# One 512-column matmul of the high weights on high and low tokens side by side, for the MLP up and FFN gate and up products of two transformer blocks

## The chip, the cores and the metric

The kernel runs on one NeuronCore of a Trainium2 chip. The metric is the device time of one execution in microseconds (us), smaller is better. TensorE (PE; its weight loads are listed as PEld), VectorE (DVE), ScalarE (ACT), GpSimd (POOL) and the DMA queues (SP issues nearly all weight loads) work side by side, each through its own instructions in program order, and wait for each other by semaphores.

## What is computed

Two blocks in a row on 256 tokens of width 1024, everything in float32. The first block has two layers, each an attention and a squared-ReLU MLP; the second has a SwiGLU feed-forward (FFN), a hybrid mixer and a second FFN.

```python
# first block, for each of 2 layers (D = 1024, F = 4096)
h = h + merge_heads(attention(...)) @ w_o
h = h + jnp.square(jax.nn.relu(rms_norm(h, g) @ w_up)) @ w_down
# second block (F2 = 2816); sh, sc, g: rows of c_act @ w_ada + b_ada (9 of them)
h = modulate(rmsnorm(x, n1), sh1, sc1)
x = x + 0.5 * g1 * ((jax.nn.silu(h @ w_gate) * (h @ w_up)) @ w_down)      # FFN 1
x = x + g2 * hybrid_mixer(modulate(rmsnorm(x, n2), sh2, sc2), ...)
x = x + 0.5 * g3 * (swiglu with other weights of the same shapes)          # FFN 2
return rmsnorm(x, norm_final)
```

## The kernel before

**Products.** Every float32 operand is split into two float32r parts, high and low, and a product is made in three passes that add up in one PSUM bank: high by high, high weights by low tokens, low weights by high tokens. `by_token` (L216, with `part`, L209) gives the result by token: the tokens stand still in the array and 512 columns of weights move, three matmuls of 512 columns for each block of 128 rows. `by_feature` (L233) gives it transposed: 128 columns of the weights stand still and the 256 tokens move, three matmuls of 256 columns (L245, L246, L247) for each block of rows k and each 128 columns n.

**MLP and FFN.** `hidden` (L799) goes through the hidden columns in cuts. For cut j, `up` makes the hidden activations; then the down products of cut j-1 follow (`by_token`), so that one cut's activations are made by the other engines while PE multiplies the one before. The MLP has 8 cuts of 512 columns (L415). After the up product of a cut, for each of its two banks: ScalarE's ReLU (L839), VectorE's square (L841), ScalarE's high part (L259), VectorE's low part (L260). The FFN has a cut of 512 columns made by token, one of 256, and four of 512 (L416); for each bank ScalarE makes the SiLU of the gate (L1092), VectorE the product with the up part (L1102), and then high (L259) and low part (L260).

**Weights.** `plan` lists all weight slabs (128 partitions x 1024 values, 512 KB) in the order of their use. SP loads them into 5 raw buffers. `prepare` (L155) splits each: ScalarE writes the high part (L174, or L178 with a gain for the MLP's up weights), VectorE (for some slabs GpSimd) the low part (L175, L179), into 5 pairs of buffers; PE frees those, the split frees the raw buffer. `take(i)` (L184) emits, at the place where the program uses slab i, the splitting of up to four slabs behind it. So up to four slabs behind the one in use are split ahead, and the instructions that make a cut's hidden activations stand in the queues of ScalarE and VectorE behind the splitting of the slabs of the down products that follow, and ahead of that of the next cut's up slabs. Between the slabs stand 72 slabs of `w_ada` for the second block's modulation, spread over the two MLPs and FFN 1 and 2 at a rate per slab (`plan_hidden`, L400): VectorE adds each up in two instructions (L485), and GpSimd adds over the partitions after every fourth (L490).

**PSUM.** Two pools of four banks: `acc` (down products, projections) and `mm` (up products, transposes, attention).

**Side chains.** Small chains of work (`start`, `tick`) go on between the products; `setup2` (L944) loads small inputs through GpSimd's queue and, 12 ticks later, transposes them (`fill_columns`, L907).

Below, M0 and M1 are the two MLPs, F1 and F2 the two FFNs.

Of the kernel before, what the change touches and what calls it, by code (L numbers as in the profile page):

```python
# [16 lines left out]
S = 256  # L17
# [4 lines left out]
TP = 128  # L22
# [6 lines left out]
def kernel(ctx: ExitStack, tc: tile.TileContext, a: dict, out: bass.AP):  # L29
# [28 lines left out]
    BUFS = {"x": 4, "q": 12, "m": 10, "ra": 3, "rb": 6, "pr": 3, "pT": 4, "gm": 3, "rr": 1}  # L58
# [75 lines left out]
    def load_ahead(most=RB):  # L134
        while at["dma"] < min(len(plan), at["prep"] + most):
# [12 lines left out]
            else:  # L148
                # the first product waits for no more than it needs
# [34 lines left out]
    def take(i):  # L184
        """Slab i, and more made ready behind it."""
# [19 lines left out]
    def by_t(xT, t):  # L205
        """The stationary operands of token tile t: [(hi, lo)] by k."""
        return [(x[0][:, j, tok(t)], x[1][:, j, tok(t)]) for x in xT for j in range(4)]

    def part(p, xs, ws, first, last):  # L209
        """p += x @ w, by token."""  # L210
# [5 lines left out]
    def by_token(idx, xs, ps, first=True, last=True, token_first=False, after=None, before=None):  # L216
        """ps[t] += x[t] @ slab; xs[t]: [(hi, lo)] by k."""
# [15 lines left out]
    def by_feature(idx, xT, ps, before=None):  # L233
        """ps: [128, 2, 256] each; (x @ w)^T, by blocks of 128 columns of w."""
        k = 0
        for i in idx:
            if before is not None:
                before(k)
            for wh, wl in take(i):
                xh, xl = (z[:, k % 4, :] for z in xT[k // 4])  # L240
# [30 lines left out]
    def transposed(bl, tag):  # L271
        """Up to 4 [128, 128] blocks, transposed and split; returns [(hi, lo)] by block."""
# [27 lines left out]
    def mean_square(parts, n, eps=EPS):  # L300
        """mean of squares along the free axis, plus eps."""
# [18 lines left out]
    def warm(func):  # L320
        """Has ScalarE load the table of a function ahead of its use."""
# [9 lines left out]
    def log1p_of(e, shape):  # L331
        """log(1 + e) for 0 <= e <= 1, as 2 atanh(e / (2 + e))."""
# [23 lines left out]
    def columns(n, parts, queue):  # L356
        """Rows of 128 values as columns: [128, n]."""
# [15 lines left out]
    def keep_warm(n):  # L373
        """TensorE's clock is at half speed until it has been busy for some microseconds."""
# [25 lines left out]
    def plan_hidden(ups, w_down, cuts, rate, early=0, after=0):  # L400
        """Weights of the cuts of a hidden layer; each cut's last product is one step behind its first ones."""
        up, down = [], []
        for j in range(len(cuts) + 1):
# [5 lines left out]
            if j > 0:  # L409
                c0, n = cuts[j - 1]  # L410
# [1184 lines left out]
```

## Time and profile before

| | us |
|---|---|
| median of 3 runs | 1217.19 |
| lowest, highest | 1216.63, 1222.46 |
| span of the profiled execution | 1219.5 |
| PE busy in it | 1174.3 (96%) |
| DVE, ACT, POOL busy | 865.2, 650.9, 304.3 |
| DMA queue of the weights, share of 16 engines | 59.7% |

The page gives one profiled execution: its span, the busy time of each engine, the span in slices, the chain of work that ended last, and the costliest groups of instructions. Matmuls overlap in the array, so a matmul's listed duration is longer than its share of the time; what one costs is read from the distance between starts. The order of stages in the span is attention 0 (to 130), M0 (130 to 318), attention 1, M1 (446 to 628), F1 (631 to 822), the mixer, F2 (1022 to 1211).

### The profile page before, as it was taken

Reading aid. Unit: us, or ns where it says so; the run is one execution under the profiler, and the core shown is the slowest. Engines: PE = TensorE matmul, PEld = TensorE weight load, DVE = VectorE, ACT = ScalarE, POOL = GpSimd, SP = SyncE. Lnnn points to the kernel's source line nnn. Section 1 sums busy time; section 2 is a strip of 40 time slices with the busy share of each in tenths; the row PEclk is TensorE's granted clock in tenths of the full one; section 3 lists DMA queues with packets and bytes.
Section 4 is the critical chain, followed back from the end, with each engine's and each line's share of the span. In section 5 each row is a group of like instructions: output and inputs, shape, how many; then the busy total and the mean of one; then the engine's idle time right before and its main releaser. Section 6 shows DMA issues by size and latency. Waiting matters only on the chain.

```text
span 1219.5 us, 19985 instructions
## 1 busy us (share of the span) xinstructions
PE 1174.3 (96%) x7669; PEld 1059.2 (87%) x7669; DVE 865.2 (71%) x1218; ACT 650.9 (53%) x1115; POOL 304.3 (25%) x260
## 2 busy tenths in 40 slices
PE   8999999999999999999989999998998999999997
PEld 8977989988899789989878999988987787899996
DVE  6665678887677568778777877756776776766445
ACT  6565665445555665455545444545765564444443
POOL 3054202133002511211153112154136405111002
PEclk9999999999999999999989999999998999999999
DMA  8642467886553347878846888853632263777650
GB/s 277 194 127 99 157 226 236 274 275 223 184 172 123 105 130 235 288 264 299 284 143 214 292 268 312 276 176 118 220 89 88 93 226 111 270 232 228 222 189 36
DMA packets 128479, 243.04 MB, mean 199 GB/s; under 512 B 8515, under 2 KB 16612, under 8 KB 128384
## 3 DMA queue, kind: packets, MB, share of 16 engines
q1 hardware_dynamic: 126688, 239.96, 59.7%
q0 software_dynamic: 1376, 1.28, 0.5%
q8 instruction: 60, 0.98, 0.3%
q10 hardware_dynamic: 320, 0.53, 0.1%
q14 instruction: 35, 0.29, 0.1%
HBM read 240.65 MB, written 1.09 MB: 198 GB/s over the span
## 4 chain that ended last, share of the span: by engine, by line
PE 64%; DVE 16%; ACT 6%; DMA 6%; issue 5%; POOL 3%; SPq 0%; POOLq 0%; ACTq 0%; DVEq 0%
PE mm L247 8%; PE mm L246 8%; PE mm L245 8%; PE acc L212 7%; PE acc L213 7%; PE acc L214 7%; DVE wl L179 4%; DMA raw<-in_w_down_dram 3%; PE acc L245 3%; PE acc L247 3%; PE acc L246 3%; DVE wl L175 2%; ACT wh L174 2%; PE mm L213 2%; PE mm L212 2%
## 5 line engine op out<-in xcount | busy, mean ns | idle before, releaser
L174 ACT CAST wh<-raw 128x1024 fp32r<-128x1024 f32 (+1 forms) x231 | 237.7, 1041 | 221.0 <-DMA raw<-in_w_down_dram 67.2
L175 DVE TENSOR_TENSOR wl<-raw,wh 128x1024 fp32r<-128x1024 f32 (+1 forms) x193 | 257.8, 1350 | 137.2 <-ACT wh L174 134.8
L247 PE MATMUL mm<-xh,wl 128*128 128x256 f32 x1088 | 309.3, 284 | 4.4 <-DVE wl L179 4.3
L245 PE MATMUL mm<-xh,wh 128*128 128x256 f32 x1088 | 309.1, 284 | 0.1
L246 PE MATMUL mm<-xl,wh 128*128 128x256 f32 x1088 | 308.4, 283 | 0.0
L179 DVE SCALAR_TENSOR_TENSOR wl<-raw,cols,wh 128x512 fp32r<-128x512 f32 (+1 forms) x270 | 204.0, 806 | 68.0 <-ACT wh L178 64.5
L247 PEld LDWEIGHTS mm<-xh,wl 128*128 128x128 f32 x1088 | 209.3, 192 | 5.9 <-DVE wl L179 5.9
L245 PEld LDWEIGHTS mm<-xh,wh 128*128 128x128 f32 x1088 | 209.3, 192 | 1.3 <-ACT wh L178 0.6
L246 PEld LDWEIGHTS mm<-xl,wh 128*128 128x128 f32 x1088 | 209.3, 192 | 0.7
L178 ACT ACTIVATE wh<-raw,cols 128x512 fp32r<-128x512 f32 (+1 forms) x270 | 175.3, 708 | 64.5 <-PE acc L246 20.1
L212 PE MATMUL acc<-wh,mh 128*128 128x512 f32 x524 | 207.6, 396 | 0.0
L213 PE MATMUL acc<-wl,mh 128*128 128x512 f32 x524 | 205.4, 392 | 0.0
L214 PE MATMUL acc<-wh,ml 128*128 128x512 f32 x524 | 205.1, 391 | 0.0
L490 POOL PARTITION_ALL_REDUCE ada<-ada x18 | 66.4, 3690 | 352.1 <-DVE ada L485 153.4
L175 POOL TENSOR_TENSOR wl<-raw,wh 128x1024 fp32r<-128x1024 f32 (+1 forms) x38 | 91.4, 2407 | 138.9 <-ACT wh L174 132.3
L214 PEld LDWEIGHTS acc<-wh,ml 128*128 128x128 f32 x524 | 99.0, 189 | 21.1
L212 PEld LDWEIGHTS acc<-wh,mh 128*128 128x128 f32 x524 | 98.9, 189 | 20.8 <-issue 1.7
L213 PEld LDWEIGHTS acc<-wl,mh 128*128 128x128 f32 x524 | 99.1, 189 | 19.0 <-DVE wl L175 0.2
L485 DVE SCALAR_TENSOR_TENSOR ada<-raw,c_act,ada 128x512 f32<-128x512 f32 x144 | 107.7, 748 | 2.5
L245 PE MATMUL acc<-xh,wh 128*128 128x256 f32 x352 | 102.0, 290 | 0.0
L246 PE MATMUL acc<-xl,wh 128*128 128x256 f32 x352 | 99.5, 283 | 0.0
L247 PE MATMUL acc<-xh,wl 128*128 128x256 f32 x352 | 99.5, 283 | 0.0
(318 smaller groups left out, 1673.5 us busy)
## 6 DMA issues: line engine op xcount, KB each, us to landing
raw<-in_w_ada_dram SPq DMA_DIRECT2D x72, 512.0 KB, 5.4
raw<-in_w_up_dram SPq DMA_DIRECT2D x64, 512.0 KB, 4.9
raw<-in_w_down_dram SPq DMA_DIRECT2D x64, 512.0 KB, 5.7
raw<-in_ffn_w_gate_dram SPq DMA_DIRECT2D x44, 512.0 KB, 4.7
raw<-in_ffn_w_up_dram SPq DMA_DIRECT2D x44, 512.0 KB, 4.7
raw<-in_ffn_w_down_dram SPq DMA_DIRECT2D x44, 512.0 KB, 5.2
raw<-in_moba_w_qkv_dram SPq DMA_DIRECT2D x23, 512.0 KB, 5.0
raw<-in_w_in_dram SPq DMA_DIRECT2D x20, 512.0 KB, 4.1
```

The source lines that it names most:

```text
L174: ACT.copy(hi, raw)
L175: (POOL if i in on_pool else DVE).tensor_tensor(lo, raw, f(hi), op=OP.subtract)
L178: ACT.mul(hi[:, k], raw[:, k], gain[k])
L179: DVE.scalar_tensor_tensor(out=lo[:, k], in0=raw[:, k], scalar=gain[k], in1=f(hi[:, k]), op0=OP.mult, op1=OP.subtract)
L212: PE.matmul(p, lhsT=xh, rhs=wh, start=first and n == 0, stop=False)
L213: PE.matmul(p, lhsT=xh, rhs=wl, start=False, stop=False)
L214: PE.matmul(p, lhsT=xl, rhs=wh, start=False, stop=last and n == len(ws) - 1)
L245: PE.matmul(o, lhsT=wh[:, c], rhs=xh, start=k == 0 and n % 2 == 0, stop=False)
L246: PE.matmul(o, lhsT=wh[:, c], rhs=xl, start=False, stop=False)
L247: PE.matmul(o, lhsT=wl[:, c], rhs=xh, start=False, stop=k == 7 and n % 2 == 1)
L485: DVE.scalar_tensor_tensor(out=acc, in0=raw[:, i, :], scalar=c_act[:, k:k + 1], in1=acc, op0=OP.mult, op1=OP.add)
L490: POOL.partition_all_reduce(acc, acc, TP, ReduceOp.add)
```

## The change

MLP and FFN cuts use a new `by_halves` in place of `by_feature`: high and low tokens lie side by side in one tile, so that one matmul of 512 columns multiplies the high weights with both, into both halves of a whole bank; a matmul of 256 columns adds the low weights by high tokens to the second half. The two halves are added when they are read (`sums`): ScalarE copies the second half to SBUF, VectorE adds the first to it, for 128 hidden columns at a time. A product of 512 columns so needs four banks in place of two. Around it:

- the MLP's square and the FFN's product of gate and up move to GpSimd, and ReLU and SiLU read SBUF;
- the FFN's cuts after the first are all of 256 columns (nine), so that gate and up fit the four `mm` banks; their slabs are 4 blocks of 256 columns; the down products of the last two cuts are made together (`hidden_order`);
- the first cut of an MLP and the second of an FFN use `acc` banks;
- `setup2` starts in attention 0 and transposes when M0 begins.

```diff
-    BUFS = {"x": 4, ...}
+    BUFS = {"x": 2, ...}
...
+    def by_halves(idx, xT, ps, before=None):
+        k = 0
+        for i in idx:
+            if before is not None:
+                before(k)
+            for wh, wl in take(i):
+                x = xT[k // 4][:, k % 4]
+                for n, p in enumerate(ps):
+                    c = slice(n * TP, (n + 1) * TP)
+                    PE.matmul(p, lhsT=wh[:, c], rhs=x, start=k == 0, stop=False)
+                    PE.matmul(p[:, 1, :], lhsT=wl[:, c], rhs=x[:, 0, :], start=False, stop=k == 7)
+                k += 1
+                if k % 2:
+                    tick()
+            done(i)
+            tick()
+
+    def sums(ps, name):
+        got = []
+        for i in range(0, len(ps), 2):
+            u = sb("ra", (TP, 2, S), name=name)
+            for j in range(2):
+                ACT.copy(u[:, j, :], ps[i + j][:, 1, :])
+            for j in range(2):
+                DVE.tensor_tensor(u[:, j, :], ps[i + j][:, 0, :], u[:, j, :], op=OP.add)
+            got.append(u)
+        return got
...
     def new_xT():
-        return [pair("x", (TP, 4, S)) for _ in range(2)]
+        return [sb("x", (TP, 4, 2, S), F32R, "xT") for _ in range(2)]
...
+    def hidden_order(cuts):
+        n = len(cuts)
+        if cuts[-1][1] == 512:
+            return [[j - 1] if j else [] for j in range(n + 1)]
+        return [[j - 1] if 0 < j < n - 2 else [] for j in range(n - 1)] + [[n - 3], [n - 2, n - 1]]
...
-    FFN_CUTS = [(0, 512), (2560, 256)] + [(j * 512, 512) for j in range(1, 5)]
+    FFN_CUTS = [(0, 512)] + [(512 + j * 256, 256) for j in range(9)]
...
     def mlp(...):
-            ps = [mm_ps((TP, 2, S)) for _ in range(2)]
+            ps = [(mm_ps if j else acc_ps)((TP, 2, S)) for _ in range(4)]
...
-            by_feature(ids[0], xT, ps, before)
+            by_halves(ids[0], xT, ps, before)
...
-            for p in ps:
-                r = sb("ra", (TP, 2, S), name="relu")
-                ACT.activation(out=r, in_=p, func=AF.Relu)
+            for u in sums(ps, "up"):
                 q = sb("rb", (TP, 2, S), name="sq")
-                DVE.tensor_tensor(q, r, p, op=OP.mult)
+                ACT.activation(out=u, in_=u, func=AF.Relu)
+                POOL.tensor_tensor(q, u, u, op=OP.mult)
                 hT += hidden_part(q)
...
     def ffn(...):
+            banks = acc_ps if j == 1 else mm_ps
+            ps = [banks((TP, 2, S)) for _ in range(2)]
+            by_halves(ids[0], xT, ps)
+            sg, = sums(ps, "sg")
+            ACT.activation(out=sg, in_=sg, func=AF.Silu)
...
+            ps = [banks((TP, 2, S)) for _ in range(2)]
+            by_halves(ids[1], xT, ps)
             finish(*pending)
+            u, = sums(ps, "up")
+            q = sb("rb", (TP, 2, S), name="gu")
+            POOL.tensor_tensor(q, sg, u, op=OP.mult)
+            return hidden_part(q)
...
-    attention_layer(0, A0, xT, vs, chains, nxt[3])
+    attention_layer(0, A0, xT, vs, chains, nxt[3], lambda: start(setup2()))
```

## Rows read from the trace of the kernel before

**Rows 1.** The page's head: span and instructions, busy us of each engine (share).

```profile
span 1219.5 us, 19985 instructions
PE 1174.3 (96%) x7669; PEld 1059.2 (87%) x7669; DVE 865.2 (71%) x1218; ACT 650.9 (53%) x1115; POOL 304.3 (25%) x260
```

**Rows 2.** Timeline of PE, one cut of M0: start us, us, engine, line, operands.

```profile
209.63 0.28 PE L245 MATMUL mm<-xh,wh 128*128 128x256 f32 x1
...
221.15 0.40 PE L212 MATMUL acc<-wh,mh 128*128 128x512 f32 x1
...
232.05 0.28 PE L245 MATMUL mm<-xh,wh 128*128 128x256 f32 x1
```

**Rows 3.** Costliest groups: xcount, then busy us, mean ns, idle before.

```profile
L245 PE MATMUL mm<-xh,wh 128*128 128x256 f32 x1088 | 309.1, 284 | 0.1
```

**Rows 4.** Windows of M0 (two), F1, F2: length, then busy us by engine.

```profile
209.60:232.10 22.50, 22.50 (x146) 20.57 (x145) 19.52 (x25) 11.90 (x18) 3.17 (x3) 1.00 0.79 269
255.20:279.40 24.20, 23.07 (x145) 20.43 (x143) 19.48 (x24) 11.43 (x18) 4.51 (x2) 1.00 0.79 261
...
744.70:778.60 33.90, 33.90 (x241) 32.05 (x240) 27.98 (x31) 16.05 (x19) 4.93 (x3) 1.00 0.88 311
...
1132.10:1166.00 33.90, 33.90 (x241) 32.04 (x240) 17.26 (x16) 14.71 (x16) 0.00 (x0) 1.00 0.62 200
```

**Rows 5.** Waits of PE, 232 to 300 (M0), then 480 to 606 (M1).

```profile
PE mm L247 <- DVE wl L179: 3.5, 4, 1.7
...
PE mm L247 <- DVE wl L179: 0.8, 2, 0.5
```

**Rows 6.** Timeline of DVE: first square of cuts 2 and 6, M0, then M1.

```profile
178.36 0.68 DVE L841 TENSOR_TENSOR sq<-relu,mm 128x512 f32<-128x512 f32 x1
...
275.44 0.68 DVE L841 TENSOR_TENSOR sq<-relu,mm 128x512 f32<-128x512 f32 x1
...
492.88 0.68 DVE L841 TENSOR_TENSOR sq<-relu,mm 128x512 f32<-128x512 f32 x1
...
589.45 0.68 DVE L841 TENSOR_TENSOR sq<-relu,mm 128x512 f32<-128x512 f32 x1
```

**Rows 7.** Timeline of DVE: the hidden activations of one cut of M0.

```profile
225.47 0.68 DVE L841 TENSOR_TENSOR sq<-relu,mm 128x512 f32<-128x512 f32 x1
226.84 0.70 DVE L260 TENSOR_TENSOR ml<-sq,mh 128x512 fp32r<-128x512 f32 x1 [0.69 <-ACT mh L259]
...
229.43 0.75 DVE L485 SCALAR_TENSOR_TENSOR ada<-raw,c_act,ada 128x512 f32<-128x512 f32 x1
```

**Rows 8.** Groups by form: the nearest operations to the new ones (busy us, mean ns).

```profile
L839 ACT ACTIVATE relu<-mm 128x512 f32<-128x512 f32 x32 | 19.0, 593 | 3.8 <-PE mm L247 3.8
L259 ACT CAST mh<-sq 128x512 fp32r<-128x512 f32 x32 | 19.9, 621 | 37.0 <-DVE sq L841 37.0
L259 ACT CAST mh<-mm 128x256 fp32r<-128x256 f32 x18 | 6.3, 374 | 11.6 <-PE mm L641 9.4 <-PE mm L265 2.1
L260 DVE TENSOR_TENSOR ml<-mm,mh 128x256 fp32r<-128x256 f32 x18 | 7.1, 417 | 17.9 <-ACT mh L259 17.9
L542 POOL TENSOR_TENSOR pr<-pr,rs 128x512 f32<-128x512 f32 x24 | 24.9, 1042 | 89.6 <-DVE rs L541 89.6
```

**Rows 9.** Timeline, F1: gate-by-up products of two cuts; PE's end of the latter cut.

```profile
736.13 0.67 DVE L1102 TENSOR_TENSOR gu<-sg,mm 128x512 f32<-128x512 f32 x1
...
771.73 0.68 DVE L1102 TENSOR_TENSOR gu<-sg,mm 128x512 f32<-128x512 f32 x1
...
767.73 0.40 PE L212 MATMUL acc<-wh,mh 128*128 128x512 f32 x1
```

**Rows 10.** Groups by form, DVE, 682 to 800 (F1): idle before, and on whom.

```profile
L175 DVE TENSOR_TENSOR wl<-raw,wh 128x1024 fp32r<-128x1024 f32 x43 | 59.2, 1395 | 22.8 <-ACT wh L174 22.7
```

**Rows 11.** Timeline of POOL: a step of attention 0; the first load of `setup2`.

```profile
98.70 1.03 POOL L542 TENSOR_TENSOR pr<-pr,rs 128x512 f32<-128x512 f32 x1
...
130.36 0.60 POOL L946 DMA_DIRECT2D b_ada<-in_b_ada_dram  x1 [0.29 <-POOL b_ada L945]
```

More of the change, by code (lines that the diff above doesn't have):

```diff
@@ L205, in by_t @@
     def by_t(xT, t):
-        return [(x[0][:, j, tok(t)], x[1][:, j, tok(t)]) for x in xT for j in range(4)]
+        return [(x[:, j, 0, tok(t)], x[:, j, 1, tok(t)]) for x in xT for j in range(4)]
     def part(p, xs, ws, first, last):
@@ L239, in by_feature @@
             for wh, wl in take(i):
-                xh, xl = (z[:, k % 4, :] for z in xT[k // 4])
+                xh, xl = (xT[k // 4][:, k % 4, e, :] for e in range(2))
                 for n in range(2 * len(ps)):
@@ L402, in plan_hidden @@
         up, down = [], []
-        for j in range(len(cuts) + 1):
+        for j, made in enumerate(hidden_order(cuts)):
             mixed["rate"] = rate if after < j < len(cuts) - 1 else 0.0
@@ L408, in plan_hidden @@
                            for i, (w, g) in enumerate(ups)])
-            if j > 0:
-                c0, n = cuts[j - 1]
+            if made:
+                c0, n = cuts[made[0]][0], sum(cuts[i][1] for i in made)
                 down.append([slab(w_down, c0, n // TP, s * 512, 512) for s in range(2)])
@@ L653, in heads_attention, with attention_layer @@
         return run()
-    def attention_layer(layer, ids, xT, vs, chains, next_chain):
+    def attention_layer(layer, ids, xT, vs, chains, next_chain, between=lambda: None):
         rstd, rrow = [], []
@@ L802, in hidden @@
         acc = [[None, None], [None, None]]
-        made = None
+        made = []
         ups, downs = plans
-        for j in range(len(cuts) + 1):
-            new = up(j, ups[j]) if j < len(cuts) else None
+        downs = list(downs)
+        for j, some in enumerate(hidden_order(cuts)):
+            if j < len(cuts):
+                made.append(up(j, ups[j]))
             if j == 1:
                 acc = [[acc_ps() for _ in range(2)] for _ in range(2)]
-            if 0 < j < len(cuts):
+            if not some:
+                continue
+            hT = sum((made[i] for i in some), [])
+            down = downs.pop(0)
+            if downs:
                 for s in range(2):
-                    apart = tail is not None and j == len(cuts) - 1 and s == 1
-                    by_token(downs[j - 1][s], by_block(made), [acc[t][s] for t in range(2)], first=j == 1,
-                             last=(lambda t, n: t == 1 and n == len(downs[j - 1][s]) - 1) if apart else False)
-            elif j == len(cuts):
+                    apart = tail is not None and len(downs) == 1 and s == 1
+                    by_token(down[s], by_block(hT), [acc[t][s] for t in range(2)], first=some[0] == 0,
+                             last=(lambda t, n: t == 1 and n == len(down[s]) - 1) if apart else False)
+            else:
                 if tail is not None:
                     update(1, 1, acc[1][1])
-                token_first(downs[j - 1], by_block(made), acc, False, lambda t, s: update(t, s, acc[t][s]),
-                            order, tail)
-            made = new
+                token_first(down, by_block(hT), acc, False, lambda t, s: update(t, s, acc[t][s]), order, tail)
     def mlp(layer, plans, xT, vs, chains, next_chain, between=lambda j: None, order=BY_HALF):
@@ L855, in forget_bias @@
         for k in range(8):
-            xh, xl = (z[:, k % 4, :] for z in xT[k // 4])
+            xh, xl = (xT[k // 4][:, k % 4, e, :] for e in range(2))
             PE.matmul(p, lhsT=wf[0][:, k], rhs=xh, start=k == 0, stop=False)
@@ L913, in fill_columns @@
             r += m
-        yield 12
+        if go is None:
+            yield 12
+        else:
+            while not go:
+                yield 1
         p = mm_ps((TP, r))
```

29 lines of the change are left out of this document (7 added, 22 removed).

## The prediction

> **What bounds the kernel now.** I began with the page's head. PE is busy for 1174.3 of 1219.5 us and the other engines far less [rows 1], which looks as if any PE time saved were saved for good. But matmuls overlap, so a busy PE may still be held up, and the average covers stages of several kinds. So I read PE's timeline next: in an ordinary cut of M0 the 96 up matmuls take 221.15 - 209.63 = 11.52 us, 0.1200 us each, and the 48 down matmuls 232.05 - 221.15 = 10.90 us, 0.2271 us each [rows 2]. A cut is 22.4 us of PE.
>
> Then the windows: in M0 VectorE is busy for 19.5 of such a cut's 22.5 us, and a later cut takes 24.2 us [rows 4]. PE's waits say why: from 232 to 300 it waits for VectorE's low parts of the up weights, in M1 a little too [rows 5]. The square of the first bank of a cut is a mark that VectorE passes once a cut. From cut 2 to cut 6 of M0 it takes (275.44 - 178.36) / 4 = 24.27 us a cut, in M1 (589.45 - 492.88) / 4 = 24.14 [rows 6]. PE needs 22.4. So in both MLPs the preparation of weights (load, ScalarE, VectorE, back to the raw buffer) is slower than PE by 1.8 us a cut. It lives on the slabs that it has ahead, and PE waits when these are used up. In F1 the mark is the gate-by-up product: 771.73 - 736.13 = 35.6 us for a cut of 512 columns, of which PE needs 33.9; at 771.73 VectorE is 4.0 us behind PE's end of that cut, and PE does not wait yet [rows 4, 9]. In F2 VectorE is busy for 17.3 of 33.9 us and PE alone sets the pace [rows 4]. The reader should see from this that M0, M1 and F1 have two limits nearly equal, and that a change which takes from PE and gives to VectorE's chain is paid where the chain is late.
>
> **The change part by part.** *Matmuls.* A pair of one row block and 128 columns costs 3 x 0.1200 = 0.3600 us; the new one 0.2271 + 0.1200 = 0.3471, so 0.0129 less [rows 2]. There are 1088 such pairs in the MLPs and FFNs [rows 3]: 256 in M0, 256 in M1, 288 in each FFN's columns after the first cut (8 x 4 x 8; 9 x 2 x 8 for gate and for up). The work of PE falls by 14.0 us: 3.3, 3.3, 3.7, 3.7. No row shows a matmul of 512 followed by one of 256 on the same bank for long; between the two shapes the starts keep their distance [rows 2], so I take the sum of the two.
>
> Here the Trainium skill speaks against the change: the page TensorE: Matmul & The Clock Gate, in the section on why the gap is 56 and not 53.3 ns, has a fixed cost of about 2.5 ns for each warm matmul beyond its columns. By it the edit would save an estimated 1088 x 2.5 ns = 2.7 us of PE's work. The rows differ: 512 columns cost 0.2271 and 256 cost 0.1200, which is 0.1071 for 256 columns and 0.0129 besides [rows 2], and the measurement decides.
>
> *The hidden chain of the MLP.* Now, from the first square to the next instruction of other work, VectorE spends 229.43 - 225.47 = 3.96 us on a cut, waiting 0.69 us for each of two high parts [rows 7]. After the change it makes four adds of 256 columns first. Priced by the 128x256 subtraction from PSUM, 0.417 us, they last 1.67, and ScalarE's copies (128x256 cast, 0.374) run ahead of them while VectorE still splits a slab. The first ReLU waits for the second add: 0.83 + 0.59 = 1.42. Then GpSimd squares (nearest: the 128x512 product, 1.04): 2.46; high part 0.62: 3.08; low part 0.69: 3.77. ScalarE is in order, so the second ReLU follows the first high part: 3.08 + 0.59 = 3.67; square 4.71; high 5.33; low 6.02 [rows 7, 8]. VectorE's chain grows from 3.96 to 6.02, by 2.06 us a cut, though its busy time hardly grows. Queued behind its low parts are the sums for `w_ada` and the splitting of the next cut's up slabs, and PE waits for these. The load waits that VectorE has now come late in a cut, after more than five slabs, so the five raw buffers filled meanwhile do not cover the new wait. The bounds are +0.5 (ScalarE and GpSimd quicker than their nearest rows, waits partly absorbed) and +3 us a cut (each hop of a semaphore, and GpSimd behind a reduction).
>
> From cut 2 on the chain sets the pace: five chains until the first up slab of cut 7, 5 x 2.06 = 10.3 us later than now. PE arrives earlier by 3 cuts x 32 pairs x 0.0129 = 1.2, which only lengthens its wait, but the chain, which starts from PE's end of a cut, starts that much earlier; cut 7 itself gives 0.4. M0: +8.7 us. M1 by the same working: +8.7. With the bounds: 0 to +13 each.
>
> *The FFN's chain.* Now a bank costs VectorE two instructions and a wait, the same 0.68 + 0.69 + 0.60, 1.97 us. After: two adds for the gate, 0.83; two for up, 0.83; square's place taken by the product 1.04; high 0.62; low 0.69: 4.01 [rows 7, 8], that is +2.04 for each cut of 256. SiLU now waits for VectorE's adds, and the next high part of a slab for SiLU: 0 to 0.59 + 1.05 more. Against this, from 682 to 800 VectorE is idle for 22.8 us ahead of its splitting, for ScalarE that waits for loads [rows 10], and with a pause twice in six or seven loads five raw buffers can cover most of it. I take +0.4 a cut, bounds 0 and +3.7. The chain is slower than PE by (35.6 - 33.9) / 2 = 0.85 a cut of 256 already, PE gets quicker by 0.41, so it falls behind by 1.66 in each of the eight cuts with `w_ada`: 13.3, less the 4.0 that it may be behind, is a wait of 9.3; less the 3.7 saved, F1 is +5.6 us (0 to +30).
>
> *F2.* Chain and loads have room [rows 4]: -3.7 (-3.7 to +3).
>
> *Banks.* In each MLP's first cut the fourth `acc` bank is free only after the last residual update; in each FFN's second cut the down product takes banks that the sums have just read. Four hand-overs, at about one 0.68 instruction and a hop each: +3 (0 to 8). Later cuts have the down product of over 5 us between a bank's last reading and its next use; if the chain were later than that, it would cost the difference.
>
> *`setup2`.* Nine issues on GpSimd's queue at 0.60, 5.4 us, now lie in attention 0, ahead of GpSimd's products for the second half of the heads (the one at 98.70 and five after it); before they ran when GpSimd had nothing else [rows 11]. PE waits there only if the ticks between do not cover it: +1 (0 to 5).
>
> *Layout of x, order of the last two down products, ReLU and SiLU from SBUF:* the same bytes and columns on PE, ScalarE has room (11.9 of 22.5 [rows 4]): nothing, at worst 2. FFN weight rows of 1 KB in place of 2 KB may lengthen loads; that is in F1's upper bound.
>
> Sum: 8.7 + 8.7 + 5.6 - 3.7 + 3 + 1 = +23.3. On the profiled execution, 1219.5 becomes 1242.8. Its span stands 2.3 above the median of 1217.2, so on the median 1240.5.
>
> **The rivals.** *PE sets the pace throughout.* If VectorE's new waits fell into waits that it has anyway (22.8 us in F1 speaks for that), the 14.0 us would be kept but for the 3 of the banks: 1217.2 - 11 = 1206. It decides when VectorE's chain takes under 22.0 us a cut in the MLPs; 24.2 now, before anything is added, speaks against it. *The chain keeps its pace.* If the new links cost nothing net, M0, M1 and F1 stay as they are, F2 gives 3.7, and 3 go for banks: 1214 to 1217, no change. *The FFN's chain at its upper bound*: +3.7 a cut puts F1 near +25: 1260. *By the skill's rule* of 2.5 ns PE's work falls by 2.7 only, and with PE setting the pace the time is within 0.5% of now; the rows give this almost no chance.
>
> **How the numbers follow.** Forecast 0.57, FFN at its upper bound 0.15, unchanged pace 0.14, PE's pace 0.13, the skill's rule 0.01. Slower by over 0.5% (about what a measurement of this kernel can tell from no change) is 0.57 + 0.15 = 0.72, with a little off for a forecast that comes out low: 0.71. Within 0.5%: 0.16. Faster: 0.13. The range leaves out PE's pace below and the worst FFN above 1262: 1209 to 1262. The forecast's own is 1222 to 1260.
>
> **What would show it.** Right: in M0 and M1 VectorE's mark once a cut (the second add) at 26 us, PE waiting for low parts of up weights for 15 us or so in each, DVE idle for the GpSimd square and the high part twice a cut; the pair at 0.347 us; F2 shorter by about 4. Wrong: marks at 22 us a cut and no waits of PE in M0 and M1; then the new links were covered, and the PE saving is the result. If the pair takes more than 0.36, the matmuls' price was wrong, and F2 would be longer.

## The result, and the profile after

The changed kernel takes 1302.33 us (1299.66 to 1308.76, four runs) against 1216.91, a ratio of 1.0688, 95% interval 1.0665 to 1.0712. The forecast was 1240.5, the range ended at 1262: the direction was right, the size was wrong by 62 us.

The profiled execution has a span of 1307.1 us, 87.6 more than before. Its head, span and busy time of each engine:

```profile
span 1307.1 us, 18173 instructions
PE 1203.3 (92%) x6581; PEld 1020.3 (78%) x6581; DVE 879.0 (67%) x1304; ACT 690.1 (53%) x1251; POOL 355.0 (27%) x310
```

Against [rows 1], PE issues 1088 matmuls fewer and is busy for 29.0 us more; and it is idle for 1307.1 - 1203.3 = 103.8 us where it was idle for 45.2. So 58.6 of the 87.6 us are waits. The other 29.0 go with a lower clock: the mean granted clock of the execution fell from 0.984 to 0.958, which is 0.042 x 1307.1 - 0.016 x 1219.5 = 35 us of full-clock time, against the 7.6 that the cheaper matmuls save (1088 x 0.007).

Where it lies is read from PE's timeline: the times of the first and last up matmuls of the stages cut the span into pieces (us; the experiments stand in the same table). "F1, mixer" runs from the first up product of F1's first 256-column cut to the same of F2.

| | to M0 | M0: first two up products | M0: to the last up product | attention 1 | M1: all up products | M1's end, F1's first cut | F1, mixer | F2 to the end |
|---|---|---|---|---|---|---|---|---|
| before | 130.2 | 23.5 | 141.0 | 151.2 | 159.5 | 53.8 | 387.4 | 172.7 |
| after | 131.4 | 30.8 | 148.0 | 153.8 | 185.3 | 53.7 | 428.3 | 175.8 |
| e1_dve_product | 131.1 | 30.5 | 142.2 | 152.1 | 167.6 | 54.9 | 400.7 | 171.0 |
| e2_no_reduce | 133.1 | 30.6 | 149.8 | 152.0 | 174.8 | 54.1 | 408.2 | 171.0 |
| e3_before_pool_square | 128.2 | 23.5 | 144.8 | 151.2 | 181.9 | 52.5 | 385.9 | 172.7 |
| e4_late_setup2 | 129.3 | 23.8 | 150.8 | 153.7 | 186.3 | 53.8 | 428.1 | 173.2 |
| e5_before_reorder | 130.9 | 23.5 | 134.5 | 151.0 | 157.9 | 52.7 | 386.4 | 172.7 |
| e6_mended | 130.3 | 23.9 | 136.5 | 149.9 | 162.0 | 53.8 | 401.8 | 171.0 |
| e7_before_quarter | 132.0 | 23.5 | 134.5 | 150.3 | 157.9 | 53.6 | 386.9 | 172.6 |
| e8_mended_quarter | 130.3 | 23.5 | 133.4 | 150.3 | 157.1 | 54.0 | 388.3 | 170.8 |
| e9_ffn_three | 132.7 | 23.8 | 137.9 | 150.4 | 161.8 | 53.5 | 387.1 | 172.8 |
| e10_order_f2 | 130.2 | 23.5 | 134.5 | 152.0 | 157.9 | 53.8 | 384.8 | 171.0 |
| e11_quarter_three | 134.0 | 24.2 | 134.5 | 150.3 | 158.6 | 53.0 | 390.5 | 172.7 |

So the change cost 7.2 us at the start of M0, 7.0 in the rest of it, 25.8 in M1, 40.9 from F1 on, and 3.1 in F2. The time to the start of M0 can't be read so finely: it lies between 128.2 and 134.0 over the executions of both kernels.

*What went as forecast.* PE's timeline, one up product of M0 (compare [rows 2]): 32 pairs in 206.74 - 195.45 = 11.29 us, 0.353 a pair, where 0.347 was forecast and 0.360 was paid before.

```profile
195.45 0.39 PE L265 MATMUL mm<-xT,wh 128*128 128x512 f32 x1
195.67 0.28 PE L266 MATMUL mm<-xT,wl 128*128 128x256 f32 x1
195.79 0.40 PE L265 MATMUL mm<-xT,wh 128*128 128x512 f32 x1
...
206.74 0.40 PE L212 MATMUL acc<-wh,mh 128*128 128x512 f32 x1
```

VectorE's timeline, the chain of one cut of M0, and the first sum of cuts 2 and 6 of M0 and M1 (compare [rows 6, 7]):

```profile
184.05 1.49 DVE L281 TENSOR_TENSOR up<-mm,up 128x256 f32<-128x256 f32 x4
187.41 0.69 DVE L291 TENSOR_TENSOR ml<-sq,mh 128x512 fp32r<-128x512 f32 x1 [1.88 <-ACT mh L290]
189.71 0.69 DVE L291 TENSOR_TENSOR ml<-sq,mh 128x512 fp32r<-128x512 f32 x1 [1.61 <-ACT mh L290]
190.32 1.54 DVE L522 SCALAR_TENSOR_TENSOR ada<-raw,c_act,ada 128x512 f32<-128x512 f32 x2
...
289.23 1.41 DVE L281 TENSOR_TENSOR up<-mm,up 128x256 f32<-128x256 f32 x4
...
515.16 1.41 DVE L281 TENSOR_TENSOR up<-mm,up 128x256 f32<-128x256 f32 x4
...
625.84 1.41 DVE L281 TENSOR_TENSOR up<-mm,up 128x256 f32<-128x256 f32 x4
```

The chain takes 190.32 - 184.05 = 6.27 us (forecast 6.02), and M0 runs at (289.23 - 184.05) / 4 = 26.3 us a cut (forecast 26). In M1 it is (625.84 - 515.16) / 4 = 27.7: there is something more.

*What did not.* GpSimd's timeline in F1, with the two FFN products (L1145) that follow reductions over the partitions (L527):

```profile
716.00 0.71 POOL L531 DMA_DIRECT2D mod<-ada  x1 [0.29 <-POOL ada L527]
725.00 1.27 POOL L1145 TENSOR_TENSOR gu<-sg,up 128x512 f32<-128x512 f32 x1 [8.29 <-issue]
741.30 3.25 POOL L527 PARTITION_ALL_REDUCE ada<-ada  x1 [15.03 <-DVE ada L522]
744.84 0.71 POOL L531 DMA_DIRECT2D mod<-ada  x1 [0.29 <-POOL ada L527]
753.25 1.28 POOL L1145 TENSOR_TENSOR gu<-sg,up 128x512 f32<-128x512 f32 x1 [7.70 <-issue]
```

Between the reduction's write to memory and the next product GpSimd stands still for 7.70 and 8.29 us, waiting for nothing ("issue"). The timeline of VectorE and ScalarE around 725 shows who pays:

```profile
716.84 0.74 DVE L281 TENSOR_TENSOR up<-acc,up 128x256 f32<-128x256 f32 x2
726.31 0.62 ACT L290 CAST mh<-gu 128x512 fp32r<-128x512 f32 x1 [10.95 <-POOL gu L1145]
726.96 0.69 DVE L291 TENSOR_TENSOR ml<-gu,mh 128x512 fp32r<-128x512 f32 x1 [9.37 <-ACT mh L290]
```

The sums are ready at 717.58, the product could start then, and starts 7.4 us later. VectorE is in order: the low part waits 9.37 us for the high part, and the splitting of all later slabs stands behind it. Over F1's nine products these delays (product's start less end of the last sum) are 7.4, 1.9, 6.7, 0.1, 0.4, 1.9, 3.1, 0.1, 0.1 us. In M1 it happens twice, here once, 4.0 us after ReLU's end at 597.83:

```profile
597.20 0.63 ACT L881 ACTIVATE up<-up 128x512 f32<-128x512 f32 x1 [0.87 <-DVE up L281]
601.84 1.03 POOL L882 TENSOR_TENSOR sq<-up 128x512 f32<-128x512 f32 x1 [10.79 <-issue]
603.55 0.69 DVE L291 TENSOR_TENSOR ml<-sq,mh 128x512 fp32r<-128x512 f32 x1 [5.72 <-ACT mh L290]
```

What stands between is visible when the instructions of one line are listed: at the reduction's line and the products' lines GpSimd's sequencer has pairs of MODIFY_POOL_CONFIG.

```profile
L527 POOLq MODIFY_POOL_CONFIG  x36: 1/11/37, 189.0 to 1170.8; - x36
L882 POOLq MODIFY_POOL_CONFIG  x14: 37/37/37, 199.4 to 623.3; - x14
L1145 POOLq MODIFY_POOL_CONFIG  x12: 37/37/37, 716.8 to 854.3; - x12
```

And at the reduction's line of the kernel before:

```profile
L490 POOLq MODIFY_POOL_CONFIG  x14: 9/19/37, 151.7 to 1090.4; - x14
```

So there were 7 changes to a reduction before, and there are 18 now. From the first configuration at an FFN product, at 716.8, to that product at 725.00 are some 8.2 us. The Trainium skill has a cause for this: the page GPSIMD Engine Reference, section 2.1 Instruction dispatch, says that such an instruction can bring new code into the engine and that the first call of freshly loaded code pays about 6 us with no instruction of its own in the profile. The trace agrees in kind, with 8.2 us here; no run sees the loading itself.

*The clock.* PE's timeline in F1, the first matmuls of pairs:

```profile
781.64 0.79 PE L265 MATMUL mm<-xT,wh 128*128 128x512 f32 x1 [6.72 <-ACT wh L174]
784.38 0.63 PE L265 MATMUL mm<-xT,wh 128*128 128x512 f32 x1
785.02 0.63 PE L265 MATMUL mm<-xT,wh 128*128 128x512 f32 x1
...
789.02 0.40 PE L265 MATMUL mm<-xT,wh 128*128 128x512 f32 x1
789.37 0.40 PE L265 MATMUL mm<-xT,wh 128*128 128x512 f32 x1
```

After the wait a pair costs 0.64 us in place of 0.35. The windows of these two stretches, with the granted clock behind the busy times:

```profile
781.60:786.60 5.00, 3.39 (x9) 2.60 (x10) 4.93 (x7) 2.06 (x3) 0.00 (x0) 0.50 0.41 122
786.90:790.80 3.90, 3.90 (x25) 3.40 (x24) 3.87 (x6) 2.40 (x6) 0.00 (x0) 1.00 1.01 336
```

A wait of 6.7 us is followed by 5 us at half the clock (1.2 GHz of 2.4). So this wait was paid twice, and the prediction's sum priced every wait once.

*The start of M0.* ScalarE's and PE's timelines:

```profile
135.20 1.28 ACT L1018 ACT_TABLE_LOAD   x1
...
138.87 0.23 ACT L1019 ACTIVATE sin<-ang 128x32 f32<-128x32 f32 x1 [2.17 <-DVE ang L1016]
...
139.82 1.28 ACT L1023 ACT_TABLE_LOAD   x1
...
141.24 0.57 ACT L290 CAST xT<-mm 128x512 fp32r<-128x512 f32 x1
...
142.59 0.80 PE L265 MATMUL acc<-xT,wh 128*128 128x512 f32 x1 [3.98 <-DVE xT L291]
143.40 0.63 PE L265 MATMUL acc<-xT,wh 128*128 128x512 f32 x1
144.04 0.63 PE L265 MATMUL acc<-xT,wh 128*128 128x512 f32 x1
```

This is the rest of `setup2`, which now runs as soon as its transposes are made: two table loads and a wait of 2.17 us for VectorE stand on ScalarE ahead of the cast of M0's last tokens. PE waits 3.98 us and then runs at half the clock.

### The profile page after: what moved, and what is told of

It is laid out like the page before. It is cut to its first block, busy times and chain, and to the rows that moved or that the text cites. A ratio compares the mean times of both kernels' runs of the same rounds, so it can differ in the third digit from the quotient of the medians.

```text
span 1307.1 us, 18173 instructions
## 1 busy us (share of the span) xinstructions
PE 1203.3 (92%) x6581; PEld 1020.3 (78%) x6581; DVE 879.0 (67%) x1304; ACT 690.1 (53%) x1251; POOL 355.0 (27%) x310
## 4 chain that ended last, share of the span: by engine, by line
PE 41%; DVE 18%; issue 16%; DMA 9%; ACT 8%; POOL 8%; SPq 0%; POOLq 0%; ACTq 0%; DVEq 0%
PE mm L265 8%; PE mm L266 4%; PE acc L212 4%; DVE wl L179 4%; PE acc L213 4%; PE acc L214 4%; DVE wl L175 4%; DMA raw<-in_w_down_dram 3%; PE acc L245 3%; PE acc L246 2%; PE acc L247 2%; DVE ada L522 2%; ACT wh L174 2%; DMA raw<-in_w_up_dram 2%; POOL sq L882 2%
## 5 line engine op out<-in xcount | busy, mean ns | idle before, releaser
L265 PE MATMUL mm<-xT,wh 128*128 128x512 f32 x960 | 361.6, 416 | 31.5 <-ACT wh L178 16.7
L175 DVE TENSOR_TENSOR wl<-raw,wh 128x1024 fp32r<-128x1024 f32 (+1 forms) x193 | 251.0, 1325 | 95.0 <-ACT wh L174 93.1
L266 PE MATMUL mm<-xT,wl 128*128 128x256 f32 x960 | 282.3, 294 | 20.1 <-DVE wl L175 10.9
L265 PEld LDWEIGHTS mm<-xT,wh 128*128 128x128 f32 x960 | 191.3, 199 | 81.9 <-ACT wh L178 19.6
L179 DVE SCALAR_TENSOR_TENSOR wl<-raw,cols,wh 128x512 fp32r<-128x512 f32 (+1 forms) x270 | 196.0, 777 | 67.7 <-ACT wh L178 64.1
L266 PEld LDWEIGHTS mm<-xT,wl 128*128 128x128 f32 x960 | 192.2, 200 | 28.6 <-DVE wl L175 15.0
L178 ACT ACTIVATE wh<-raw,cols 128x512 fp32r<-128x512 f32 (+1 forms) x270 | 175.0, 707 | 64.0 <-PE acc L246 20.1
L175 POOL TENSOR_TENSOR wl<-raw,wh 128x1024 fp32r<-128x1024 f32 (+1 forms) x38 | 91.0, 2398 | 122.0 <-ACT wh L174 115.6
L522 DVE SCALAR_TENSOR_TENSOR ada<-raw,c_act,ada 128x512 f32<-128x512 f32 x144 | 119.3, 829 | 5.0 <-DMA raw<-in_w_ada_dram 2.4
L245 PE MATMUL acc<-xT,wh 128*128 128x256 f32 x352 | 101.9, 290 | 0.0
L527 POOL PARTITION_ALL_REDUCE ada<-ada x18 | 62.3, 3459 | 145.0 <-DVE ada L522 89.7
L246 PE MATMUL acc<-xT,wh 128*128 128x256 f32 x352 | 99.5, 283 | 0.0
L247 PE MATMUL acc<-xT,wl 128*128 128x256 f32 x352 | 99.5, 283 | 0.0
L882 POOL TENSOR_TENSOR sq<-up 128x512 f32<-128x512 f32 x32 | 33.3, 1040 | 179.5 <-ACT up L881 144.6
L1145 POOL TENSOR_TENSOR gu<-sg,up 128x512 f32<-128x512 f32 x18 | 23.1, 1283 | 186.2 <-DVE up L281 145.0
```

The source lines that it names most:

```text
L175: (POOL if i in on_pool else DVE).tensor_tensor(lo, raw, f(hi), op=OP.subtract)
L178: ACT.mul(hi[:, k], raw[:, k], gain[k])
L179: DVE.scalar_tensor_tensor(out=lo[:, k], in0=raw[:, k], scalar=gain[k], in1=f(hi[:, k]), op0=OP.mult, op1=OP.subtract)
L245: PE.matmul(o, lhsT=wh[:, c], rhs=xh, start=k == 0 and n % 2 == 0, stop=False)
L246: PE.matmul(o, lhsT=wh[:, c], rhs=xl, start=False, stop=False)
L265: PE.matmul(p, lhsT=wh[:, c], rhs=x, start=k == 0, stop=False)
```

## The experiments

Ratios are of medians to the kernel before on the same chip, with the 95% interval. Theory S is the turn-round of GpSimd, theory C the prediction's own: a longer chain, mis-sized.

**e1: the products back on VectorE.**

```diff
-                POOL.tensor_tensor(q, u, u, op=OP.mult)
+                DVE.tensor_tensor(q, u, u, op=OP.mult)
...
-            POOL.tensor_tensor(q, sg, u, op=OP.mult)
+            DVE.tensor_tensor(q, sg, u, op=OP.mult)
```

> The changed kernel with the MLP's square and the FFN's product of gate and up back on VectorE; everything else of the change stays. Theory S (the change's time goes to GpSimd: after each partition reduction of w_ada GpSimd needs about 8 us before its next ordinary instruction starts, and the product of a cut now stands there, with VectorE's low part and all its splitting behind it): F1 loses its waits of 7.4, 6.7, 3.1, 1.9 and 1.9 us, M1 its two of 4.0, so 25 to 30 us directly and about as much again in clock and emptied buffers: 1235 to 1265. Theory C (the step of the prediction: the chain copy, add, ReLU, product, high, low is simply longer than it was priced, and GpSimd is only one link of it): the link becomes 0.36 us shorter, twice a cut, so 6 to 12 us less in all: 1288 to 1297.

Measured: 1252.03, ratio 1.0275 (1.0242 to 1.0308): 50 us of the 85 are gone with two words. As S expected, far from C. VectorE's waits for high parts, in F1 of the changed kernel and then of e1 (us in total, times, longest):

```profile
DVE ml L291 <- ACT mh L290: 37.2, 8, 9.4
```

```profile
DVE ml L291 <- ACT mh L290: 5.5, 8, 0.7
```

**e2: the same queue on GpSimd, without the reductions.**

```diff
-            POOL.partition_all_reduce(acc, acc, TP, ReduceOp.add)
+            for _ in range(3):
+                POOL.tensor_tensor(acc, acc, acc, op=OP.add)
```

> The changed kernel with each reduction over the partitions on GpSimd replaced by three additions of the same tile (about 3.1 us in place of 3.3): the sum over the partitions is left out. GpSimd's queue keeps its length and its order, and the square and the product stay on GpSimd, but it never has to go between two kinds of work. Theory S: the wait of the first product after each reduction falls from up to 8.9 us to under 3, F1 is 25 to 40 us shorter, F2 3 to 7, M1 5 to 12: 1245 to 1275. Theory Q (the product just stands behind a long instruction in GpSimd's queue) and theory C: nothing changes, 1295 to 1303.

Measured: 1271.41, ratio 1.0429 (1.0385 to 1.0474): 31 us less, within what S expected, against Q and C. Its trace has no MODIFY_POOL_CONFIG at the lines of the additions and the products. The three additions even take longer than the reduction did (4.14 against 3.25 us), and yet the product behind them starts as soon as the sums are there (in F1 1.1 us later once, else at once). GpSimd's timeline in F1:

```profile
748.02 4.14 POOL L528 TENSOR_TENSOR ada<-ada 128x512 f32<-128x512 f32 x3 [11.36 <-DVE ada L522]
...
754.52 1.28 POOL L1146 TENSOR_TENSOR gu<-sg,up 128x512 f32<-128x512 f32 x1 [1.53 <-DVE up L281]
```

So the reduction's length and the place in the queue cost next to nothing, and the turn-round costs some 31 us. By stages (table): 20.1 from F1 on, 10.5 in M1, 4.8 in F2. F1 gives less than the 25 to 40 expected. One more rival is out by the same run: a reduction also holds up VectorE (the subtraction L175 at 766.02 of the changed kernel lasts 3.25 us beside the reduction at 765.95, and 1.22 otherwise), but VectorE's busy time is 885.8 us in e2 and 879.0 in the changed kernel, so e2 isn't faster because VectorE is held less. The 19 us that e1 gives beyond e2 go with GpSimd as a link: VectorE waits 1.88 and 1.61 us for the high parts of a cut of M0 with GpSimd in the chain, 0.69 and 0.69 in e1. No run splits these 19 us further.

**e3: GpSimd's square alone, in the kernel before.**

```diff
-                DVE.tensor_tensor(q, r, p, op=OP.mult)
+                POOL.tensor_tensor(q, r, r, op=OP.mult)
```

> The kernel before with one edit: the MLP's square is made by GpSimd from the ReLU in SBUF, in place of VectorE. Theory S: in M0 and M1, which have four to five reductions each, the square meets GpSimd's turn-round, and both stages, paced by VectorE's chain at 24.2 us a cut, get longer: 1228 to 1250. Theory C: two links per cut are 0.4 to 0.6 us longer each, seven cuts in two layers, partly absorbed: 1219 to 1231.

Measured: 1245.29, ratio 1.0222 (1.0186 to 1.0258), as S expected: this one edit, with no new matmul and no sums, costs 27 us, 22.4 of them in M1. GpSimd's timeline in M1, and ScalarE's and PE's waits there:

```profile
565.44 3.25 POOL L490 PARTITION_ALL_REDUCE ada<-ada  x1 [11.77 <-DVE ada L485]
...
578.40 1.03 POOL L841 TENSOR_TENSOR sq<-relu 128x512 f32<-128x512 f32 x1 [8.71 <-issue]
```

```profile
ACT mh L259 <- POOL sq L841: 38.9, 14, 9.9
```

```profile
PE mm L245 <- ACT wh L178: 14.5, 4, 9.1
```

M0, with five reductions too, lost only 3.8: there ReLU was ready 11 to 12 us after the end of the reduction in three of the five cuts, and the square followed it at once. How much a turn-round costs depends on where in a cut a reduction falls.

**e4: the rest of `setup2` later.**

```diff
         yield from fill_columns(cols2, by_row, first_mlp)
+        yield 12
```

> The changed kernel with one delay put back: after its transposes at the start of M0 the rest of the side chain (position angles, sine and cosine with two table loads on ScalarE) waits 12 more steps, so that it no longer stands ahead of the last cast of M0's tokens. Theory P (the move of this chain cost the start of M0: PE waits 4.0 us for the low tokens, and its clock is at half for some us after): M0's first cut is 4 to 8 us shorter and the kernel 1294 to 1299. Rival: M0 is paced by VectorE's chain from cut 2 on, and a later first cut only used up slack: 1300 to 1304.

Measured: 1300.11, ratio 1.0675 (1.0639 to 1.0712), which can't be told from the changed kernel. Both theories have their part. The first two up products of M0 take 23.8 us in place of 30.8, so the moved chain did cost 6.9 there (23.5 before). But the rest of M0 is 2.8 longer, since the chain of VectorE sets its pace from cut 2 on and the earlier start only makes PE wait later; and M1 is 1.0 longer.

**e5: another order of the same work, in the kernel before.**

```diff
-            for p in ps:
-                r = sb("ra", (TP, 2, S), name="relu")
-                ACT.activation(out=r, in_=p, func=AF.Relu)
-                q = sb("rb", (TP, 2, S), name="sq")
-                DVE.tensor_tensor(q, r, p, op=OP.mult)
-                hT += hidden_part(q)
...
+            for r, p in zip(rs, ps):
+                ACT.activation(out=r, in_=p, func=AF.Relu)
+            for q, r, p in zip(qs, rs, ps):
+                DVE.tensor_tensor(q, r, p, op=OP.mult)
+            return hidden_parts(qs)
```

`hidden_parts` makes both high parts, then both low parts; the FFN's 512-column cuts get the same order.

> The kernel before with the order of a cut's hidden activations changed and nothing else: for the two banks of an MLP cut and of a 512-column FFN cut first both ReLUs (SiLUs as before), then both products on VectorE, then both high parts, then both low parts, in place of one bank after the other. VectorE's two waits of 0.69 us for a high part in each cut then lie behind a product. Theory V (in M0 and M1 the in-order chain of VectorE sets the pace): 0.7 to 1.3 us less for each of five to seven cuts in each layer, F1 a few less: 1201 to 1211. Theory L (the loads into five raw buffers set that pace, and a shorter chain only waits longer for them): 1214 to 1219.

Measured: 1211.96 on a chip where the kernel before took 1220.29, ratio 0.9922 (0.9900 to 0.9944). The time itself lies 1 us above theory V's range and under L's; on the 1216.91 of before, for which the ranges were made, the ratio gives 1207, inside V's. VectorE's timeline of one cut of M0:

```profile
269.23 1.28 DVE L849 TENSOR_TENSOR sq<-relu,mm 128x512 f32<-128x512 f32 x2
270.61 1.29 DVE L297 TENSOR_TENSOR ml<-sq,mh 128x512 fp32r<-128x512 f32 x2
271.82 1.53 DVE L493 SCALAR_TENSOR_TENSOR ada<-raw,c_act,ada 128x512 f32<-128x512 f32 x2
```

The chain takes 271.82 - 269.23 = 2.59 us in place of 3.96 [rows 7], and its waits are gone. M0 is 6.5 us shorter, M1 1.5, and PE has no wait left in M0. So the chain did set M0's pace, as the prediction read it, and the waits for the high parts were what could be saved. In M1 it cost PE little.

**e6: the changed kernel mended** (e1, e4, and e5's order in the MLP).

```diff
-            for u in sums(ps, "up"):
-                q = sb("rb", (TP, 2, S), name="sq")
-                ACT.activation(out=u, in_=u, func=AF.Relu)
-                POOL.tensor_tensor(q, u, u, op=OP.mult)
-                hT += hidden_part(q)
...
+            us = sums(ps, "up")
...
+            for u in us:
+                ACT.activation(out=u, in_=u, func=AF.Relu)
+            for q, u in zip(qs, us):
+                DVE.tensor_tensor(q, u, u, op=OP.mult)
+            return hidden_parts(qs)
```

> The changed kernel with three things mended: products on VectorE, the side chain of the position angles 12 steps later, and in the MLP the order sums, both ReLUs, both squares, both high parts, both low parts. With products on VectorE alone it was 1252. Theory V: the late side chain gives about 4 in M0, the order 1 to 2 us a cut where the chain of VectorE sets the pace: 1234 to 1246, with M1 within 3 us of the kernel before, and what is left lies in F1. Theory B (what is left over the kernel before is made of bank hand-overs and start-up, not of the chain): 1245 to 1252.

Measured: 1230.46, ratio 1.0073 (1.0044 to 1.0101), lower than either theory said. As V expected, M1 is within 3 us of before (162.0 against 159.5) and what is left lies in F1: 401.8 against 387.4.

**e7 and e8: the preparation relieved.** Only one of four slabs of `w_ada` is loaded and added up, in the kernel before (e7) and in e6 (e8); three quarters of the modulation's sums are left out.

```diff
-    ada_order = [(None, j, half, kk) for j in range(9) for half in range(2) for kk in range(4)]
+    ada_order = [(None, j, half, kk) for j in range(9) for half in range(2) for kk in (3,)]
...
-        if kk == 0:
+        if kk == 3:
```

The rates of the plan go down with it, to 0.14, 0.13, 0.17 and 0.1 for M0, M1, F1 and F2.

> The kernel before with only the last of each four slabs of w_ada loaded and added up (18 in place of 72, the rest of the modulation is left out). VectorE has 1.5 us less for each slab left out and the loads are fewer; PE's work is the same. Theory V: M0 and M1 fall to PE's pace of 22.4 us a cut, F1 to 33.9: 1190 to 1206. Rival: PE's waits in these stages come from elsewhere (first cuts, stage changes), 1208 to 1217.

> The mended form of the changed kernel with only 18 of the 72 slabs of w_ada, as in the quarter form of the kernel before, and to be compared with that. Here the preparation should have room, so the comparison shows what the new matmuls give where PE sets the pace. From the changed kernel's rows a pair costs 0.236 + 0.117 = 0.353 us, 0.007 less than three matmuls: 1088 pairs give 7.6 us. If that is all: 5 to 9 us less than the quarter form of before. With the pair priced as in the prediction: 12 to 15 less. If the sums on VectorE, banks and short FFN cuts still cost even with room: equal or up to 12 us more.

Measured: e7 1212.13, ratio 0.9934 (0.9911 to 0.9956); e8 1209.00, ratio 0.9907 (0.9892 to 0.9921). e7 came out as the rival said. M0 falls to PE's pace (134.5, the same as by e5's order), M1 gives 1.5 only, and F1 gives nothing: 386.9 against 387.4. So in the kernel before, F1 ran at PE's pace, and all that the preparation cost PE was some 8 us. e8 is 3 us better than e7, between the first and the third of its expectations. The intervals overlap, so the gain with room on VectorE is shown by the stages only: 1.1 us in M0, 0.8 in M1 and 1.8 in F2, less 1.4 in F1; less than the 7.6 of its matmuls.

**e11: what the matmuls give.** e8 with three matmuls of 256 columns for each pair.

```diff
-                    PE.matmul(p, lhsT=wh[:, c], rhs=x, start=k == 0, stop=False)
+                    PE.matmul(p[:, 0, :], lhsT=wh[:, c], rhs=x[:, 0, :], start=k == 0, stop=False)
+                    PE.matmul(p[:, 1, :], lhsT=wh[:, c], rhs=x[:, 1, :], start=False, stop=False)
```

> The quarter form of the mended kernel (18 of 72 slabs of w_ada, PE sets the pace in M0, M1, F1, F2; it was 1209.0) with each 512-column matmul of the high weights made as two of 256 columns into the same two halves: nothing but PE's instructions differs, 1088 pairs become 1088 triples. By the pair's rows in the changed kernel (0.353 against 0.360): 5 to 10 us longer. By the prediction's price (0.347): 12 to 16 longer. By a fixed cost of 2.5 ns for a matmul: 2 to 4 longer.

Measured: 1217.77, ratio 0.9983 (0.9969 to 0.9998), 8.8 us longer than e8, which ran on another chip. In the table M0's two pieces, M1, F1 and F2 give 0.7 + 1.1 + 1.5 + 2.2 + 1.9 = 7.4. So the pair is worth 7 to 9 us, as its 0.353 says, and not the 14.0 of the prediction. The fixed cost per matmul on the Trainium skill's page TensorE: Matmul & The Clock Gate (section Wait — 56ns, not 53.3ns?) would give an estimated 2.7, and this run does not agree. Beside e7 it also shows what the rest of the change costs when PE sets the pace: with the same three matmuls, 1217.77 against 1212.13. Of these 5.6 us the table puts 3.6 in F1; 2.0 lie ahead of M0, where executions differ by that much anyhow.

**e9: the FFN without sums.** e6 with the old three matmuls and one bank for gate and for up, in the new 256-column cuts.

```diff
-            ps = [banks((TP, 2, S)) for _ in range(2)]
-            by_halves(ids[0], xT, ps)
-            sg, = sums(ps, "sg")
-            ACT.activation(out=sg, in_=sg, func=AF.Silu)
+            ps = [mm_ps((TP, 2, S))]
+            by_feature(ids[0], xT, ps)
...
+            ACT.activation(out=sg, in_=ps[0], func=AF.Silu)
...
```

> The mended form of the changed kernel with the old three matmuls of 256 columns and one bank for gate and for up in the FFNs, so without the copies and sums there; the cuts of 256 columns, their order and the MLPs stay as in the mended form (1230.5, of which F1 from its first 256-column cut to F2's first is 401.8 us, before 387.4). Theory A (the sums' four additions a cut, 1.7 us of VectorE and waits of SiLU for them, keep F1 behind PE): F1 falls to 386 to 391, F2 rises from 162.4 to 164 to 165, in all 1216 to 1223. Theory K (the short cuts and their slabs are what costs in F1): F1 stays at 398 to 403, in all 1229 to 1234.

Measured: 1221.55, ratio 1.0013 (0.9994 to 1.0033). As theory A expected, F1 and the mixer fall to 387.1, and F2 rises by 1.8 (to 172.8 in the table). The windows of one F1 cut, e6 and then e9 (busy time of PE, PEld, VectorE, ScalarE, GpSimd, then the clock):

```profile
731.20:752.00 20.80, 18.77 (x89) 15.51 (x88) 17.28 (x21) 8.13 (x14) 4.55 (x2) 0.92 0.82 278
```

```profile
734.00:750.90 16.90, 16.90 (x121) 15.98 (x120) 15.07 (x16) 6.97 (x9) 4.55 (x2) 1.00 0.79 265
```

VectorE is busy for 17.28 us in this cut of e6, more than the 16.8 that PE needs for one (e8's F1 and F2 cuts), and for 15.07 without the sums. But over six cuts of F1, the second to the seventh of 256 columns (679.0 to 789.6 in e6, 683.0 to 785.4 in e9), it is 15.4 and 13.7 on average, so its work alone is not the bound. The sums also add a link: ScalarE's SiLU waits for VectorE's sums of the gate, and the high parts of later slabs stand behind it in ScalarE's queue. This wait in the six cuts of e6 (us in total, times, longest):

```profile
ACT sg L1146 <- DVE sg L281: 16.4, 6, 3.9
```

In e9 there is none. In e8, with the same sums and banks but fewer slabs of `w_ada`, it is 6.5 us, and the cuts keep PE's 16.8. So the sums with their copies put F1 behind PE where the preparation is full; how much of it is the link and how much VectorE's work, no run separates. The short cuts and their 1 KB rows cost nothing that is seen.

**e10: the change where there is room.** e5, with the new matmuls, sums and short cuts (and VectorE's product) in F2 alone.

```diff
-    ffn(F1, late["ffn1"][0], late["ffn1"][1], mods[2], lambda t, s: late["mix"][2](t, s), ahead2)
+    ffn(F1_CUTS, F1, late["ffn1"][0], late["ffn1"][1], mods[2], lambda t, s: late["mix"][2](t, s), ahead2)
...
-    ffn(F2, late["ffn2"][0], late["ffn2"][1], lambda: mods[8], go_last, ahead4, tail)
+    ffn(FFN_CUTS, F2, late["ffn2"][0], late["ffn2"][1], lambda: mods[8], go_last, ahead4, tail)
```

`F1_CUTS` are the FFN cuts of the kernel before, made by `by_feature`; F2's are made by `by_halves`, with 0.4 slabs of `w_ada` a slab in place of 0.3.

> The kernel before with the new order of a cut's hidden activations (which alone gave 1212.0), and the new matmuls, sums and short cuts in F2 alone, where VectorE and the loads have room; product on VectorE. F2 was 164.2 us from its first 256-column cut to the end before and 162.4 in the mended form. Theory R (the change pays only where VectorE has room): F2 1.5 to 2.5 us shorter, 1208 to 1211. Rival: the sums add as much at F2's end as PE saves: 1211 to 1214.

Measured: 1208.74, ratio 0.9905 (0.9883 to 0.9927), as R expected. F2 takes 171.0 in place of 172.7. It is faster than both kernels; against e5 the intervals overlap, and the 1.7 us of F2 are shown by the stage only.

## Why the prediction failed

**The step that failed** is in the MLP's hidden chain, "Then GpSimd squares (nearest: the 128x512 product, 1.04)", and in the FFN's, "square's place taken by the product 1.04". The duration was near (1.03 for the square, 1.27 for the FFN's product). What was missing is that GpSimd also makes the reductions, and that it can't go from one to the other at once. The row of 1.04 came from attention 0 [rows 8], where GpSimd makes a row of products and no reduction comes between. The trace of before did show the price, in a place that cost nothing there (GpSimd, M1):

```profile
476.87 3.64 POOL L490 PARTITION_ALL_REDUCE ada<-ada  x1 [27.98 <-DVE ada L485]
489.59 1.53 POOL L493 TENSOR_SCALAR ada<-ada 1x512 f32<-1x512 f32 x1 [9.09 <-issue]
```

The scaling of the reduced row needs nothing but the reduction, and starts 9.09 us after its end. The bound for GpSimd ("+3 us a cut", with "GpSimd behind a reduction" in it) should have been read from this row: up to 9 us for a cut with a reduction. The worth of the step: 31 us by e2, 50 together with all else that GpSimd as a link costs (e1).

**The clock.** No term of the sum held it. PE's clock was at half after the waits of 4.0 and 6.7 us shown above, and also from 244.1 to 250.9, around waits of 1.3 and 1.7 us with one matmul between them. In all, 58.6 us of more waiting went with 29.0 more of busy time, though the matmuls had become cheaper.

**M0's pace: right.** The chain of 6.02 us was 6.27, the 26 us a cut were 26.3 in M0, and M0 from its third cut on lost 7.0 where 8.7 were forecast (9.8 in e4, whose M0 starts undisturbed). e5 shows the same reading from the other side. M1 was forecast like M0 and lost 25.8; without the turn-round (e2) it lost 15.3, with the square on VectorE (e1) 8.1. Of what e2's 15.3 is above the 8.7, the clock is a part: PE's was at 0.50 from 549.8 to 556.6, an estimated 3 us for the 6.05 us that PE was busy there. No run separates the rest.

**F1: wrong by more than GpSimd.** Of 40.9 us, 20.1 go with the turn-round (e2) and 7.5 more with the product on VectorE (e1). What is left, 13.3, is still over the 5.6 of the forecast. Two errors lay under that number. F1's chain was taken to be 0.85 us a cut slower than PE before the change, from the marks of one cut [rows 9]. The marks of the cuts on either side:

```profile
705.15 0.68 DVE L1102 TENSOR_TENSOR gu<-sg,mm 128x512 f32<-128x512 f32 x1
...
801.15 0.69 DVE L1102 TENSOR_TENSOR gu<-sg,mm 128x512 f32<-128x512 f32 x1
```

The three cuts take VectorE 96.0 us and PE 96.4 (682.26 to 778.64), so the chain kept PE's pace and was only late in between; e7 says the same. And the sums were put at +0.4 a cut out of a range of 0 to 3.7, trusting 22.8 us of VectorE's waits for loads [rows 10] to absorb them. In e6 the first two of the six cuts above take 16.8 us, as PE needs, and the next four 17.9 to 20.9, so once the slabs ahead are used up the sums cost 1.1 to 4.1 a cut. e9 shows that it is the sums with their copies.

**F2.** -3.7 was forecast, 3.1 more were measured: two products there also waited, for 5.4 and 8.9 us, behind reductions. Without that it is -1.7 (e1, e2), the pair's smaller gain.

**Matmuls: over-priced.** 14.0 us were forecast, 7 to 9 measured (e11). Adding up a 512 and a 256 from streams of one shape each gave 0.347; side by side they cost 0.353.

**Banks.** +3 was put down for four hand-overs, some 0.75 each. The first two up products of M0 (e4, without the moved chain) and of M1 took 0.3 us more each, though their 64 pairs save some 0.5, so the two in the MLPs were priced about right. In the FFNs nothing is seen: in e8 the down products of the second cut take 11.0 us, as 48 matmuls do.

**`setup2`: priced by its issues.** The prediction counted nine DMA issues in attention 0 (+1; M0 begins 1.2 later, less than executions differ there) and took the transposes at M0's start for free. The whole rest of the chain came with them, two table loads included, ahead of M0's tokens: 6.9 us at that place (e4), some 4 to the end of M0.

**The range.** Its upper end stood on the FFN's chain with absorbed or unabsorbed waits. A rival for GpSimd with two kinds of work, from the row above, would have reached further up.

## What to carry to other kernels

Before work goes to GpSimd, list what else it does and look for the row where it goes from one kind of instruction to the other: idle time that waits for nothing, about 8 us here, harmless until the work stands in a chain on which an in-order engine waits. A step that is moved takes everything with it that its side chain still issues, here two table loads. And where an engine waits in its own chain, try the order first: both products before both high parts gave 8 us in a kernel on which a cleverer matmul could give at most as much.

## What the runs showed of the hardware

GpSimd needed about 8 us from its change of configuration after a partition reduction to the first ordinary instruction (716.8 to 725.00; 7.4 to 10.7 over the seven squares and products of M1 and F1 that waited for nothing else), with no busy row in the profile for it; where the operand came 11 to 12 us after the reduction's end, as in three cuts of M0 in e3, nothing of it is seen. PE's clock went to half for 5 us after a wait of 6.7 and for 5.9 after one of 4.0 (142.59 to 148.52, nine pairs, 0.64 us each after the first). A 512-column matmul followed by one of 256 with other weights into half of the same bank costs 0.353 us, 0.006 more than the two in streams of their own.
